# Two halves of an attention result leave apart and are added at the branch load; a one-column product moves from VectorE to GpSimd

## The chip, the cores and the metric

The kernel runs on one core of one Trainium2 chip. The metric is the device time of one execution, in microseconds. Of the kernel before, three runs gave 1775.21, 1780.83 and 1787.9 us; the median is 1780.83 us. One execution was profiled.

In the rows below PE is TensorE (matrix products), PEld its weight load, DVE is VectorE, ACT is ScalarE, POOL is GpSimd and SP is SyncE, whose queue issues nearly all transfers. L734 is line 734 of the kernel before.

## The reference, cut to what matters

One inference step of a one-layer encoder, for a prompt of 1024 tokens and a sample of 64 tokens: a norm and an input projection, stick-breaking attention beside a state-space branch, a gated merge of the two, an output projection, a gated feed-forward and an embedding stage. The change lies in the attention and where its result enters the merge:

```python
def _sb_block(qb, start, k, v, q_offset):
    z = jnp.einsum('bqhd,bkhd->bhqk', qb, k) * (SB_HEAD_DIM ** -0.5)
    ...
    visible = s_pos[None, :] < t_pos[:, None]
    log_keep = jnp.where(visible, jax.nn.log_sigmoid(-z), 0.0)
    after = lax.cumsum(log_keep, axis=3, reverse=True) - log_keep
    w = jnp.where(visible, jnp.exp(jax.nn.log_sigmoid(z) + after), 0.0)
    return jnp.einsum('bhqk,bkhd->bqhd', w, v)
...
merged = (jax.nn.sigmoid(g_attn) * (o_attn @ W['w_branch_attn'])
          + jax.nn.sigmoid(g_ssm) * (o_ssm @ W['w_branch_ssm']))
```

So a weight is sigmoid(z) times the product of sigmoid(-z) over all later visible keys. There are 8 heads of 64 columns each.

## The kernel before, in words

All matrix products are made in pieces: an operand is split into a high part (a ScalarE copy to a rounded type) and a low part (a VectorE subtraction), by `split` (L124 to L126) or `unit` (L102 to L115), and three products are added (`mm3_iter`, L137 to L139).

**Heads.** `head` walks the 1024 queries of one head in four groups `i2` of 256, each made of two tiles `i` of 128. The visible keys of groups 2 and 3 are taken in two parts, the later keys first. For each tile and part, `stick` lets ScalarE make p = sigmoid(-z) and w = sigmoid(z) from PSUM (L728, L729), VectorE scan p backwards into a running product (L730), and then w be multiplied by p shifted by one column (L732), on GpSimd for tile 0 and on VectorE for tile 1. The last column of a second part is multiplied by the carry, the running product of the part before it: a product of 128 partitions by one column, on VectorE (L734). The carry is a copy of column 0 of p (L737). `decode` does the same for the 64 sample tokens against 2048 cached keys, in five steps for each pair of heads, all of whose L732 are GpSimd's. In all there are 48 such one-column products: 32 of heads, 16 of `decode`.

The weights are then transposed by TensorE (L776) and split into wth and wtl (L780, L781). `weigh` (L806) multiplies them by values whose high and low parts lie side by side as 128 columns, so that a group's result `av` in PSUM has the high part's product in partitions 0 to 63 and the low part's in 64 to 127. ScalarE copies the upper half to `ot` (L719, from L792), VectorE adds it to the lower half into `o` (L793), and SP's queue writes `o` to the scratch `oad` of that pair of heads (L794). This happens 32 times. `av` has one PSUM bank, which `decode` uses too.

**Branch.** `branch` reads `oad` of one pair back (L918) into `braw`, a tile with one buffer, and splits it into `ba`. `early` does so for pairs 0 to 2 while the last heads run, each as one load of 1088 columns; `merge` does it for pair 3 in three chunks `CH` of 364, 362 and 362 columns, and then multiplies by the branch weights.

**Order.** A string, `ORDER`, written by a rule with fixed times, says in which order the heads, `decode` ("d"), the projections of the next pairs ("p"), the gate products that have no part in the attention ("g", `fill`) and `early` ("E") are put down. 48 further steps of gate products follow the last head. Matrix products of the fill may be held behind a given score product (`hold`). Within this, a planner that simulates the times of the engines (`schedule_with_timeline_sim=True`) fixes the order of the instructions on each engine; SP's queue, like each engine's, is worked off in that order.

Of the kernel before, what the change touches and what calls it, by code (L numbers as in the profile page):

```python
# [8 lines left out]
F32 = mybir.dt.float32  # L9
# [3 lines left out]
OP = mybir.AluOpType  # L13
# [4 lines left out]
SEQ = 1024  # L18
DEC = 64
TOK = SEQ + DEC  # L20
# [8 lines left out]
CH = ((0, 364), (364, 362), (726, 362))  # L29
# [39 lines left out]
class Net:  # L69
# [653 lines left out]
    def stick(self, P, z, n, carry, more, e):  # L723

        nc = self.nc
        w = P.tile([128, 512], F32, "w", "w")[:, :n]
        p = P.tile([128, 512], F32, "p", "p")[:, :n]
        nc.scalar.activation(p, z, AF.Sigmoid, scale=-1.0)  # L728
        nc.scalar.activation(w, z, AF.Sigmoid)  # L729
        nc.vector.tensor_tensor_scan(p[:, ::-1], p[:, ::-1], self.zero.to_broadcast([128, n]),  # L730
                                     1.0 if carry is None else carry, op0=OP.mult, op1=OP.add)
        (nc.gpsimd if e == 'g' else nc.vector).tensor_tensor(w[:, :n - 1], w[:, :n - 1], p[:, 1:], op=OP.mult)  # L732
        if carry is not None:
            nc.vector.tensor_tensor(w[:, n - 1:], w[:, n - 1:], carry, op=OP.mult)  # L734
        if more:
            carry = P.tile([128, 1], F32, "cy", "cy")
            nc.vector.tensor_copy(carry, p[:, 0:1])  # L737
        return w, carry

    def head(self, P, j, h, qs, ks, vs):  # L740

        nc = self.nc
        for i2 in range(4):
            nb = 2 * (i2 + 1)
            av = None
            parts = []
            carry = [None, None]
            m = (0, 0, 2, 4)[i2]
            for b0, b1 in ((m, nb), (0, m)) if m else ((0, nb),):
                ws = []  # L750
                for i in range(2):
                    qi = 2 * i2 + i
                    e1 = min(b1, qi + 1)
                    c0, n = b0 * 128, (e1 - b0) * 128
                    z = self.ps.tile([128, 512], F32, name="z", tag="z")[:, :n]
                    q = qs[:, qi * 128:(qi + 1) * 128]
                    last = b1 == nb
                    for r in range(2):
                        mile = nc.tensor.matmul(z, q, ks[:, r, c0:c0 + n], start=r == 0, stop=r == 1 and not last)
                    self.miles.append(mile)  # L760
                    if last:
                        nc.tensor.matmul(z[:, n - 128:], self.identb, self.neg, start=False, stop=True)
                    w, carry[i] = self.stick(P, z, n, carry[i], b0 > 0, EH[i])
                    ws.append(w)
                parts.append((b0, b1, ws))
            av = self.ps.tile([128, 512], F32, name="av", tag="av")[:, :256]
            done, late = 0, None
            for s0, s1, ws in parts:
                for b0 in range(s0, s1, 2):
                    ps = self.ps.tile([128, 512], F32, name="tr", tag="tr")  # L770
                    last = b0 + 2 == nb
                    for b in range(b0, b0 + 2):
                        for i, w in enumerate(ws):
                            if b <= 2 * i2 + i:
                                c = (b - b0) * 256 + i * 128
                                nc.tensor.transpose(ps[:, c:c + 128], w[:, (b - s0) * 128:(b - s0 + 1) * 128], self.ident)  # L776
                    wh = P.tile([128, 512], F32R, "wth", "wth")
                    wl = P.tile([128, 512], F32R, "wtl", "wtl")
                    for a, b in ((0, 256), (384, 512)) if last else ((0, 512),):
                        nc.scalar.activation(wh[:, a:b], ps[:, a:b], AF.Copy)  # L780
                        nc.vector.tensor_sub(wl[:, a:b], ps[:, a:b], wh[:, a:b])  # L781
                    todo = [late, (b0, last, wh, wl)]
                    if b0 + 2 < s1:
                        late = todo.pop()
                    else:
                        late = None
                    for x in todo:
                        if x:
                            done = self.weigh(av, vs, x, nb, done)
            ot = P.tile([64, 256], F32, "ot", "ot")  # L790
            o = P.tile([64, 256], F32, "o", "o")
            self.copy(EO, ot, av[64:128])  # L792
            nc.vector.tensor_add(o, av[:64], ot)  # L793
            nc.sync.dma_start(self.oad[j][h * 64:h * 64 + 64, i2 * 256:(i2 + 1) * 256], o)  # L794
            yield

    def weigh(self, av, vs, x, nb, done):
# [58 lines left out]
    def attention(self, P, PA, fill, early):  # L856

        self.oad = [self.dram.tile([128, TOK], F32, name=f"oad{j}") for j in range(4)]
        ops, self.miles = {}, []
        pa = PA.__enter__()  # L860
        for _ in self.project_pair(P, pa, 0, ops):
# [49 lines left out]
        yield from self.fm_iter(self.I["w_in"][0], n0, 8, evac, unit=unit)  # L911


    def branch(self, P, k, raw, chunks):

        b = P.pool.tile([128, 2, TOK], F32R, name=f"ba{k}")
        for c0, n in chunks:
            self.nc.sync.dma_start(raw[:, c0:c0 + n], self.oad[k][:, c0:c0 + n])  # L918
            self.split(b[:, 0, c0:c0 + n], b[:, 1, c0:c0 + n], raw[:, c0:c0 + n])
        return b  # L920

    def merge(self, P, B, raw):
        nc = self.nc

        def gates(m):
# [2 lines left out]
                nc.sync.dma_start(g[i], self.gd[8 * i + m])  # L928
            return g
        G = gates(0)  # L930
        B = B + [self.branch(P, 3, raw, CH)]
        for m in range(8):
            ga, gs = G
            if m < 7:
# [536 lines left out]
def body(tc, I, O, dbg=None, upto=99):  # L1471
    with ExitStack() as ctx:
# [58 lines left out]

        def early():

            p = pools(tc, "mrgA", dict(braw=1))
            mA.append(p)
            P = p.__enter__()
            for k in range(3):
                raw = P.tile([128, TOK], F32, "braw", "braw")
                Braw.append(N.branch(P, k, raw, ((0, TOK),)))

        PAA = pools(tc, "attA", dict(hl=2, qb0=1, qs0=2, raw=1, vs0=2, vn0=1, ob=2, kn0=1))
        with pools(tc, "att", dict(qs1=2, vs1=2, vn1=1, kn1=1, qb1=1, ks=3, w=6, p=3, cy=6, wth=2, wtl=2,
                                   ot=1, o=1, od=1, kr=1, vc=1, kk=1, wtd=1), "right") as P:
            N.ps.alias = {}
            N.attention(P, PAA, fill, early)
            with N.hold(1):
                fill(48)
# [7 lines left out]
        with pool("wout", "right") as PW:  # L1555
            N.HS = PW.tile([128, 8, 2 * DEC], F32R, name="HS")
            with pools(tc, "mrgB", dict(braw=1, ga=2, gs=2)) as P:
                raw = mA[0].tile([128, TOK], F32, "braw", "braw")
                N.merge(P, Braw, raw)
                U = N.mix_slabs(PW, 0, WO)  # L1560
            mA[0].__exit__(None, None, None)
            with pools(tc, "mix", dict(ss=4, xo=2, xn=2, xr=2, x0=1, x1=1, t1=1, t2=1)) as P:
                U += N.mix_slabs(P.pool, WO, 8)
                N.mix_out(P, U)
# [40 lines left out]
```

## Time and profile before

| | us |
|---|---|
| median of three runs | 1780.83 |
| the profiled execution's own time | 1778.77 |
| its span, first to last instruction | 1776.6 |
| attention, from the first score product to the last head's result | about 376 to 779 |
| product with the branch weights begins | 781 |

The profile has one row for each engine with its busy time, and views that cut the span into stages, list groups of instructions, list who waited for whom, and follow the chain of work that ended last. A busy TensorE is one that has a product under way; its granted clock stands beside it as a share of full speed. What a stage is worth is read from the stage, not from the mean of the span.

### The profile page before, as it was taken

The numbers are of one execution on the slowest core, as the hardware profiler recorded it, in microseconds if no ns is written. First come the engines' busy times: TensorE is split into PE (matmuls) and PEld (weight loads), VectorE is DVE, ScalarE is ACT, GpSimd is POOL, SyncE is SP. The second block draws the span as 40 slices with busy tenths as digits, with TensorE's granted clock in tenths as the row PEclk, the third lists the DMA queues.
The fourth block names the chain that finished last, engine by engine and source line by source line (L and its number), as shares of the span: only waits on it lengthen the run. The fifth ranks groups of instructions, "written<-read, shape, count | busy, mean of one in ns | idle before, by whom it ended". The sixth has DMA issues, their size and how long they took to land.

```text
span 1776.6 us, 24710 instructions
## 1 busy us (share of the span) xinstructions
PE 1692.9 (95%) x9092; PEld 1479.3 (83%) x9092; DVE 1039.0 (58%) x1581; ACT 733.5 (41%) x1357; POOL 515.3 (29%) x446
## 2 busy tenths in 40 slices
PE   8999897999999988899998999999999999999998
PEld 6999897988888877799786788888888887888886
DVE  6437735435776777767463655555655455445674
ACT  6431134124555555643343433343333344444542
POOL 2026100012322323224230444445444313001453
PEclk9999898999999999999999999999999999999999
DMA  8352534675343342147454444445444386655332
GB/s 283 95 147 64 120 89 149 216 213 137 88 101 101 83 118 83 60 143 239 143 172 148 132 149 133 160 132 187 151 149 139 125 288 215 197 189 166 107 113 89
DMA packets 220457, 258.23 MB, mean 145 GB/s; under 512 B 25888, under 2 KB 168336, under 8 KB 220320
## 3 DMA queue, kind: packets, MB, share of 16 engines
q1 hardware_dynamic: 219680, 255.20, 46.9%
q0 software_dynamic: 656, 1.44, 0.5%
q8 instruction: 72, 1.18, 0.3%
q14 instruction: 49, 0.40, 0.1%
HBM read 165.32 MB, written 76.51 MB: 136 GB/s over the span
## 4 chain that ended last, share of the span: by engine, by line
PE 73%; DVE 12%; DMA 7%; ACT 3%; issue 3%; SPq 1%; POOL 1%; DVEq 0%; POOLq 0%; ACTq 0%
PE pj L1200 13%; PE tr L1200 6%; PE pj L137 6%; PE pj L139 6%; PE pj L138 6%; PE z L1366 3%; DVE p L730 3%; PE z L1200 3%; PE pj L1366 3%; PE z L138 2%; PE z L139 2%; PE z L137 2%; PE tr L1366 2%; PE av L806 2%; PE tr L776 1%
## 5 line engine op out<-in xcount | busy, mean ns | idle before, releaser
L137 PE MATMUL pj<-H,wh 128*128 128x362 f32 (+3 forms) x648 | 217.7, 336 | 5.9 <-DVE ql L629 3.3
L139 PE MATMUL pj<-H,wl 128*128 128x362 f32 (+3 forms) x648 | 215.1, 333 | 0.6 <-DVE wl L115 0.6
L138 PE MATMUL pj<-H,wh 128*128 128x362 f32 (+3 forms) x648 | 214.6, 331 | 0.0
L126 DVE TENSOR_TENSOR wl<-raw,wh 128x1024 fp32r<-128x1024 f32 x96 | 132.3, 1380 | 120.0 <-ACT wh L125 118.7
L732 POOL TENSOR_TENSOR w<-w,p 128x383 f32<-128x383 f32 (+4 forms) x68 | 92.7, 1372 | 312.5 <-DVE w L734 185.2
L125 ACT ACTIVATE wh<-raw 128x1024 fp32r<-128x1024 f32 x96 | 101.4, 1059 | 122.8 <-PE z L1366 45.5
L137 PEld LDWEIGHTS pj<-H,wh 128*128 128x128 f32 x648 | 122.8, 190 | 7.6 <-DVE ql L629 3.7
L139 PEld LDWEIGHTS pj<-H,wl 128*128 128x128 f32 x648 | 122.5, 189 | 1.5 <-DVE wl L115 0.8
L138 PEld LDWEIGHTS pj<-H,wh 128*128 128x128 f32 x648 | 122.7, 189 | 0.9 <-issue 0.4
L1200 PE MATMUL pj<-H,s 128*128 128x512 f32 x480 | 118.2, 395 | 0.0
L148 POOL TENSOR_TENSOR rs<-rs,mhalf 128x1 f32<-128x1 f32 (+1 forms) x54 | 32.6, 605 | 278.0 <-DVE rs L147 277.9
L1200 PEld LDWEIGHTS pj<-H,s 128*128 128x128 f32 x480 | 89.9, 188 | 21.0 <-DVE c L1233 0.3
L125 ACT ACTIVATE s<-st 128x512 fp32r<-128x512 f32 x80 | 50.3, 629 | 123.6 <-PE pj L1200 112.2
L1134 POOL TENSOR_TENSOR st<-raw 128x512 f32<-128x512 f32 x40 | 60.7, 1518 | 133.8 <-DVE H L126 54.0
L126 DVE TENSOR_TENSOR s<-st,s 128x512 fp32r<-128x512 f32 x80 | 67.8, 849 | 39.4 <-ACT s L125 38.7
L119 ACT ACTIVATE wh<-raw 128x1024 fp32r<-128x1024 f32 (+1 forms) x52 | 46.8, 899 | 94.2 <-PE av L138 48.8
L780 ACT ACTIVATE wth<-tr 128x512 fp32r<-128x512 f32 (+2 forms) x112 | 50.2, 454 | 82.4 <-PE tr L776 41.9
L781 DVE TENSOR_TENSOR wtl<-tr,wth 128x512 fp32r<-128x512 f32 (+2 forms) x112 | 55.3, 496 | 49.3 <-ACT wth L780 48.9
L115 DVE TENSOR_TENSOR wl<-raw,wh 128x1024 fp32r<-128x1024 f32 (+1 forms) x50 | 51.1, 1021 | 55.0 <-ACT wh L119 54.9
L728 ACT ACTIVATE p<-z 128x512 f32<-128x512 f32 (+4 forms) x116 | 59.1, 510 | 42.6 <-PE z L830 16.7
L730 DVE TENSOR_TENSOR_SCAN p<-p,zero 128x384 f32<-128x384 f32 (+4 forms) x68 | 73.9, 1094 | 0.2
L1200 PE MATMUL pj<-H,wh 128*128 128x512 f32 x224 | 72.7, 401 | 0.6 <-ACT H L125 0.4
(553 smaller groups left out, 4630.2 us busy)
## 6 DMA issues: line engine op xcount, KB each, us to landing
sd<-c SPq DMA_DIRECT2D x77, 256.0 KB, 3.2
raw<-sd SPq DMA_DIRECT2D x77, 256.0 KB, 2.9
raw<-in_w_in_dram SPq DMA_DIRECT2D x32, 512.0 KB, 5.3
raw<-in_w_ffn_gate_dram SPq DMA_DIRECT2D x22, 512.0 KB, 3.6
raw<-in_w_ffn_up_dram SPq DMA_DIRECT2D x22, 512.0 KB, 5.1
wd<-in_w_ffn_down_dram SPq DMA_DIRECT2D x44, 256.0 KB, 3.3
td<-wd SPq DMA_DIRECT2D x22, 512.0 KB, 3.2
raw<-td SPq DMA_DIRECT2D x44, 256.0 KB, 3.0
```

Source lines behind the costliest of these rows:

```text
L125: self.nc.scalar.activation(wh, raw, AF.Copy)
L126: self.nc.vector.tensor_sub(wl, raw, wh)
L137: self.nc.tensor.matmul(out, wh, xh, start=i == 0, stop=False)
L138: self.nc.tensor.matmul(out, wh, xl, start=False, stop=False)
L139: self.nc.tensor.matmul(out, wl, xh, start=False, stop=i == n - 1)
L728: nc.scalar.activation(p, z, AF.Sigmoid, scale=-1.0)
L730: nc.vector.tensor_tensor_scan(p[:, ::-1], p[:, ::-1], self.zero.to_broadcast([128, n]), 1.0 if carry is None else carry, op0=OP.mult, op1 ...
L732: (nc.gpsimd if e == 'g' else nc.vector).tensor_tensor(w[:, :n - 1], w[:, :n - 1], p[:, 1:], op=OP.mult)
L781: nc.vector.tensor_sub(wl[:, a:b], ps[:, a:b], wh[:, a:b])
L1134: op(t, x, y)
L1200: self.nc.tensor.matmul(out, a[i][:, k], b[j][:, k], start=start and k == i == j == 0, stop=stop and k == 3 and i == 1, skip_group_check=n ...
L1366: nc.tensor.matmul(B[b + n], x[:, 0, c], y[:, 1], start=new and p == j == 0, stop=p == 10 and j == 2, skip_group_check=not new)
```

## The change

The result of a group leaves PSUM whole, by one ScalarE copy of 128 partitions, and its two halves go to two scratch tensors by two transfers; the VectorE addition in `head` is gone. `o` has two buffers, and `ot` is gone. `branch` loads both scratch tensors and adds them, in chunks of at most 512 columns; pairs 0 to 2 are loaded in two chunks instead of one. The second scratch has no sample columns. The tile `blow` that takes the second load has one buffer. Apart from this, the one-column product L734 is issued on GpSimd.

```diff
@@ stick
         if carry is not None:
-            nc.vector.tensor_tensor(w[:, n - 1:], w[:, n - 1:], carry, op=OP.mult)
+            nc.gpsimd.tensor_tensor(w[:, n - 1:], w[:, n - 1:], carry, op=OP.mult)
@@ head
-            ot = P.tile([64, 256], F32, "ot", "ot")
-            o = P.tile([64, 256], F32, "o", "o")
-            self.copy(EO, ot, av[64:128])
-            nc.vector.tensor_add(o, av[:64], ot)
-            nc.sync.dma_start(self.oad[j][h * 64:h * 64 + 64, i2 * 256:(i2 + 1) * 256], o)
+            o = P.tile([128, 256], F32, "o", "o")
+            self.copy(EO, o, av)
+            for i in range(2):
+                nc.sync.dma_start((self.oad, self.oal)[i][j][h * 64:h * 64 + 64, i2 * 256:(i2 + 1) * 256], o[i * 64:(i + 1) * 64])
@@ attention
+        self.oal = [self.dram.tile([128, SEQ], F32, name=f"oal{j}") for j in range(4)]
@@ branch
-    def branch(self, P, k, raw, chunks):
-
+    def branch(self, P, PB, k, chunks):
+
+        raw = PB.tile([128, TOK], F32, "braw", "braw")
         b = P.pool.tile([128, 2, TOK], F32R, name=f"ba{k}")
         for c0, n in chunks:
+            m = min(n, SEQ - c0)
             self.nc.sync.dma_start(raw[:, c0:c0 + n], self.oad[k][:, c0:c0 + n])
+            low = PB.tile([128, 512], F32, "blow", "blow")[:, :m]
+            self.nc.sync.dma_start(low, self.oal[k][:, c0:c0 + m])
+            self.nc.vector.tensor_add(raw[:, c0:c0 + m], raw[:, c0:c0 + m], low)
             self.split(b[:, 0, c0:c0 + n], b[:, 1, c0:c0 + n], raw[:, c0:c0 + n])
@@ early
-            p = pools(tc, "mrgA", dict(braw=1))
+            p = pools(tc, "mrgA", dict(braw=1, blow=1))
...
-                raw = P.tile([128, TOK], F32, "braw", "braw")
-                Braw.append(N.branch(P, k, raw, ((0, TOK),)))
+                Braw.append(N.branch(P, P, k, ((0, 512), (512, TOK - 512))))
@@ pools of the attention
-                                   ot=1, o=1, od=1, kr=1, vc=1, kk=1, wtd=1), "right") as P:
+                                   o=2, od=1, kr=1, vc=1, kk=1, wtd=1), "right") as P:
```

## Rows read from the trace of the kernel before

**Rows 1.** The page: busy time, share of the span and instructions of each engine.

```profile
PE 1692.9 (95%) x9092; PEld 1479.3 (83%) x9092; DVE 1039.0 (58%) x1581; ACT 733.5 (41%) x1357; POOL 515.3 (29%) x446
```

**Rows 2.** Stages: length, busy us of each engine, clock, DMA share, GB/s.

```profile
376.00:620.00 244.00, 231.36 (x1487) 212.78 (x1487) 164.01 (x296) 124.13 (x293) 70.42 (x66) 0.99 0.44 110
620.00:766.00 146.00, 126.57 (x778) 110.89 (x778) 114.21 (x202) 83.13 (x191) 42.76 (x37) 0.93 0.31 83
766.00:790.00 24.00, 24.00 (x157) 23.98 (x156) 10.54 (x19) 7.61 (x16) 2.63 (x3) 1.00 0.52 168
```

**Rows 3.** Chain of waits, 620 to 766 us: its shares by line.

```profile
by line: DVE p L730 27.6%; issue 8.1%; PE tr L776 7.1%; PE av L806 6.1%; DVE wtl L781 5.9%; DVE w L732 5.6%; PE z L830 4.4%; PE pj L137 4.2%; PE pj L138 3.8%; PE pj L139 3.7%; ACT wth L780 2.7%; ACT p L728 2.5%; DVE wl L115 2.4%; PE tr L824
```

**Rows 4.** Chain pieces of L793 by 40 us stretches, 376 to 776: start, us, what.

```profile
489.80 0.43 DVE o L793
...
755.19 0.06 DVE o L793
```

**Rows 5.** Groups by form, ScalarE, 376 to 782: copies of 256 columns from PSUM.

```profile
L780 ACT ACTIVATE wth<-tr 128x256 fp32r<-128x256 f32 x32 | 12.6, 394 | 14.4 <-PE tr L776 14.2
L719 ACT ACTIVATE ot<-av 64x256 f32<-64x256 f32 x32 | 12.2, 382 | 17.4 <-PE av L806 17.0
```

**Rows 6.** Groups by form, VectorE, 376 to 782: busy us, mean ns | idle before.

```profile
L732 DVE TENSOR_TENSOR w<-w,p 128x511 f32<-128x511 f32 x32 | 28.2, 881 | 1.5
L793 DVE TENSOR_TENSOR o<-av,ot 64x256 f32<-64x256 f32 x32 | 13.1, 408 | 7.3 <-ACT ot L719 7.2
L734 DVE TENSOR_TENSOR w<-w,cy 128x1 f32<-128x1 f32 x48 | 12.8, 267 | 0.0
```

**Rows 7.** Chain pieces of L734 by 40 us stretches, 376 to 776.

```profile
451.00 0.13 DVE w L734
...
735.47 0.90 DVE w L734
...
765.32 0.05 DVE w L734
```

**Rows 8.** Timeline, VectorE and GpSimd around 735 us.

```profile
734.21 1.27 DVE L730 TENSOR_TENSOR_SCAN p<-p,cy,zero 128x512 f32<-128x512 f32 x1
734.40 1.96 POOL L732 TENSOR_TENSOR w<-w,p 128x511 f32<-128x511 f32 x1 [3.43 <-ACT w L729]
735.40 0.97 DVE L734 TENSOR_TENSOR w<-w,cy 128x1 f32<-128x1 f32 x1
```

**Rows 9.** Groups by form, GpSimd, whole span: its shortest kinds of instruction.

```profile
L148 POOL TENSOR_TENSOR rs<-rs,mhalf 128x1 f32<-128x1 f32 x48 | 28.5, 594 | 243.7 <-DVE rs L147 243.6
L732 POOL TENSOR_TENSOR w<-w,p 128x63 f32<-128x63 f32 x4 | 1.2, 295 | 60.7 <-DVE p L730 60.7
L1594 POOL MEMSET const-float32-0.0<- 128x1 f32 x1 | 0.1, 99 | 0.2 <-issue 0.2
```

**Rows 10.** Line L732: who waited for it; us, times.

```profile
  ACT p L728: 13.7, 15
  PEld tr L776: 8.7, 5
```

**Rows 11.** Timeline, SP's queue: two loads of early branches, one of pair 3.

```profile
694.87 0.50 SPq L918 DMA_DIRECT2D braw<-oad  x1
...
707.32 0.34 SPq L918 DMA_DIRECT2D braw<-oad  x1
...
780.74 0.32 SPq L918 DMA_DIRECT2D braw<-oad  x1
```

**Rows 12.** Busy time in the stage 620 to 766: L734 alone, then L793 alone.

```profile
620.00:766.00 146.00, 5.80 (x22) 0.93 0.31 83
...
620.00:766.00 146.00, 5.32 (x13) 0.93 0.31 83
```

**Rows 13.** Groups by form, VectorE, 376 to 782: scans of 512 columns.

```profile
L730 DVE TENSOR_TENSOR_SCAN p<-p,cy,zero 128x512 f32<-128x512 f32 x32 | 43.1, 1350 | 24.5 <-ACT p L728 24.5
L730 DVE TENSOR_TENSOR_SCAN p<-p,zero 128x512 f32<-128x512 f32 x24 | 40.6, 1692 | 0.1
```

More of the change, by code (lines that the diff above doesn't have):

```diff
@@ L911, in columns, with merge @@
         yield from self.fm_iter(self.I["w_in"][0], n0, 8, evac, unit=unit)
-    def branch(self, P, k, raw, chunks):
+    def branch(self, P, PB, k, chunks):
+        raw = PB.tile([128, TOK], F32, "braw", "braw")
         b = P.pool.tile([128, 2, TOK], F32R, name=f"ba{k}")
         for c0, n in chunks:
+            m = min(n, SEQ - c0)
             self.nc.sync.dma_start(raw[:, c0:c0 + n], self.oad[k][:, c0:c0 + n])
+            low = PB.tile([128, 512], F32, "blow", "blow")[:, :m]
+            self.nc.sync.dma_start(low, self.oal[k][:, c0:c0 + m])
+            self.nc.vector.tensor_add(raw[:, c0:c0 + m], raw[:, c0:c0 + m], low)
             self.split(b[:, 0, c0:c0 + n], b[:, 1, c0:c0 + n], raw[:, c0:c0 + n])
         return b
-    def merge(self, P, B, raw):
+    def merge(self, P, B, PB):
         nc = self.nc
@@ L930, in merge @@
         G = gates(0)
-        B = B + [self.branch(P, 3, raw, CH)]
+        B = B + [self.branch(P, PB, 3, CH)]
         for m in range(8):
@@ L1557, in body @@
             with pools(tc, "mrgB", dict(braw=1, ga=2, gs=2)) as P:
-                raw = mA[0].tile([128, TOK], F32, "braw", "braw")
-                N.merge(P, Braw, raw)
+                N.merge(P, Braw, mA[0])
                 U = N.mix_slabs(PW, 0, WO)
```

## The prediction

> **What bounds the kernel now.** I read the page's busy times first, then the stages, then the chain of waits inside the stage that the change touches. The page says that TensorE is busy 95% of the span [rows 1], and the change takes no product away, so time can come only from TensorE's gaps or from its clock. The stages say where those are: from 376 to 620 us TensorE stands still for 244.0 - 231.4 = 12.6 us, from 620 to 766 us for 146.0 - 126.6 = 19.4 us at a granted clock of 0.93, and from 766 to 790 us not at all [rows 2]. VectorE is busy 114.2 of 146 us (78%) in the slow stretch, against 67% before it [rows 2]. The chain of waits agrees: there its largest entry is VectorE's scan with 27.6%, and the four VectorE entries among those shown make 27.6 + 5.9 + 5.6 + 2.4 = 41.5% [rows 3]. So work that VectorE loses or gains counts at about four tenths in the slow stretch and at little before it.
>
> **The sum, part by part.** It is made against the profiled execution, 1778.77 us (span 1776.6), which lies 2.1 below the median of the runs, 1780.83; I add 2.1 at the end.
>
> *The addition in the head goes.* It ran 32 times at 408 ns, 13.1 us of VectorE [rows 6]. What it gives back is what it holds of the chain: ten pieces between 376 and 776 us, which together are 3.3 us [rows 4]. Behind it stood the next use of the one bank of av. The rest ran beside other work, and that stays. Bounds: 0 (the next scan or split takes its place) and 13.1. I take -3.3, since the chain shows it directly.
>
> *The copy out of PSUM takes 128 partitions instead of 64.* A copy of the same 256 columns on 128 partitions took 394 ns, the one of 64 took 382 [rows 5]: 32 x 0.012 = 0.4 us of an engine with half its time free. Nothing. `o` is written one step earlier, and with two buffers the next copy waits for no transfer.
>
> *The one-column product leaves VectorE.* 48 x 267 ns = 12.8 us [rows 6]; on the chain it has 23 pieces, together 2.9 us [rows 7]. But 21 of them are short, and two long ones make 1.35 us of the 2.9. The one at 735.40 shows what a long one is: GpSimd's product began at 734.40 while VectorE's scan ran, took 1.96 us and ended at 736.36, and VectorE's one-column product, begun at 735.40, ended at 736.37 with it [rows 8]. It did no work for 0.97 us; it waited for GpSimd. The next product of two operands on VectorE would wait there instead. I therefore count only the short pieces, 2.9 - 1.35 = 1.55, rounded to -1.6; bounds 0 and -2.9.
>
> [...]
>
> *The one-column product arrives on GpSimd.* No row shows it. The nearest is the same kind of product on 63 columns, 295 ns; a fill of one column took 99 ns, and a power on one column 594 [rows 9]. I take 0.295, the same operation with the same kinds of operand, and keep 0.099 and 0.594: 48 x 0.295 = 14.2 us of GpSimd, which is busy 113 of 390 us in the attention [rows 2], so its time is free, its order is not. Queued behind it are GpSimd's wide products, and those are waited for by ScalarE 15 times (a buffer of p comes free) and by the transposes' weight loads six times with the five shown [rows 10]. Where the column stands ahead of the wide product in the queue and cannot be done while VectorE scans, the waiter loses 0.3. I take half of the 21: 21 x 0.5 x 0.295 = +3.1. Bounds: +1.0 (0.099 each) and +6.2 (0.594 each), each at half.
>
> *The addition arrives at the branch load.* Pairs 0 to 2 get two additions each, of 512 columns; the nearest VectorE row is 128x511 from SBUF, 881 ns [rows 6]: 6 x 0.88 = 5.3 us, and 0.5 for splits cut in two, an estimate. They fall between 695 and 745 us, in the slow stretch. At 41.5% of the chain [rows 3] that is 5.8 x 0.415 = +2.4; bounds 0 and +5.8.
>
> *The tail, pair 3.* Before, the last chunk was loaded at 780.74 [rows 11]. Now the last result leaves VectorE out, which gains 0.4, sends two stores instead of one and two loads instead of one, and adds 298 columns, some 0.5. That is about 1 us late in all. TensorE has products of the other pairs and other weight columns then, and stood still for none of 24 us [rows 2]. I put nothing; without that cover, +1.
>
> *SP's queue* gets 32 stores more, and eighteen loads (twelve early, six for pair 3) where there were six. They are hidden while nothing behind them is late; the case where it is stands below.
>
> Sum: 1778.8 - 3.3 - 1.6 + 3.1 + 2.4 = 1779.4; with the 2.1, **1781 us**: no change. VectorE is freed of 25.9 us and gets 7.2 back (three additions of pair 3 included, 1.4), but little of either lies on the path that sets the end.
>
> **The rivals.**
>
> *Freed VectorE time converts (faster).* For it: the slow stretch is VectorE's by the chain, and of the two removed steps 5.8 and 5.3 us lie in it [rows 12]. If all of that counts, less the 5.8 that come in, the gain there is 5.3; if half of the other 14.8 us counts before 620 us, 7.4 more. That is 12.7 us, 1768. Everything freed at once gives 25.9 - 7.2 = 18.7, 1762. Against it: before 620 us TensorE has only 12.6 us of gaps [rows 2], and the chain shows 6 us of the two steps, not 26.
>
> *GpSimd's column gets between the scans (slower).* Mechanism: the column waits for ScalarE's w and the old carry, both ready before the scan ends; put ahead of the wide product, it begins at the scan's end, the wide product follows, and VectorE's next scan waits for both, as VectorE's short product waited for GpSimd's at 735.40 [rows 8]. Place: between L730 and L730 of the same group. For it: a scan of 512 columns behind another scan, with GpSimd running, took 1.69 us on the mean, one of a second part 1.35 [rows 13]; GpSimd's product beside a scan took 1.96 [rows 8]. Price: 48 x 0.295 = 14.2, and 32 x (1.692 - 1.350) = 10.9, so 25.1 us of VectorE; at the chain's 41.5% it is 10.4 in place of the 3.1 above: 1780.9 - 4.9 + 2.4 + 10.4 = 1789. Paid in full, 1803. It decides where the planner puts the column ahead of the wide product in most groups. [...]
>
> *SP's queue stops behind `blow` (slower).* With one buffer, each second load waits until the addition of the chunk before is done, and the loads of cached keys and weights stand behind it. Before, one early load came 12.5 us after the other, since `braw` too has one buffer [rows 11]. Five such waits instead of two; if two key loads come 5 us late each and TensorE stops for them, +10, 1791. Against it: 86 us lie between the first early load and pair 3's last [rows 11], and the 20 decode steps of the 390 us come 20 us apart, so a key load has time.
>
> That the change doesn't do what it says, that is, that GpSimd's column delays VectorE as much as VectorE's own did, is inside the first case.
>
> **How the numbers follow.** No change 0.54, freed VectorE time 0.18, the column between the scans 0.16, SP's queue 0.12. The planner lays every engine's order out anew around the moved instructions; a few us either way from that are in each case. The three runs lie 0.7% apart, so about 1%, 18 us, is what can be told from no change. Below 1763 lies the end of the first rival and a lucky order, 0.11; above 1799 the full price of the second, an SP stall that goes on, and an unlucky order, 0.13; between, 0.76. The range 1766 to 1797 takes in the bounds of the sum (1780.9 - 13.1 - 2.9 + 1.0 = 1766, and 1780.9 + 6.2 + 5.8 + 1 = 1794), most of the first rival and the two slower ones at their usual price. The likeliest case alone is 1775 to 1787.
>
> **What would show it.** VectorE's busy time falls by some 19 us; L734 stands on GpSimd 48 times at about 0.3 us; the gaps of TensorE between 620 and 766 us stay near 19 us, and the scan stays at the head of the chain. The first rival: those gaps shrink to 10 or less. The second: scans of 512 columns of second parts lengthen from 1.35 toward 1.7. The third: SP's loads in early branches have long waits, and transposes of cached keys wait for a transfer. What would make the forecast wrong: a change of order that moves the fill's products out of the slow stretch, since then its gaps lie bare.

## The result, and the profile after

The changed kernel takes 1798.8 us, the median of four runs (1798.53 to 1799.56); the kernel before took 1781.14 beside it. The ratio is 1.009, its 95% interval 1.007 to 1.0111: slower by 0.9%, just inside the 1% that I called no change. The forecast of 1781 us was wrong, by 17.8 us, and the time lies 1.8 us above the range.

The page of the kernel after, busy time by engine, against [rows 1]:

```profile
PE 1703.7 (95%) x9092; PEld 1484.9 (83%) x9092; DVE 1036.4 (58%) x1513; ACT 732.1 (41%) x1360; POOL 539.4 (30%) x494
```

VectorE has 68 instructions fewer, and is busy 2.6 us less. I had forecast 19: what was taken from VectorE did not shorten its busy time by the sum of the durations, as the groups below show.

The stages of the kernel after (columns as in [rows 2]); the third runs to the first product with the branch weights, the fourth from there to the last:

```profile
376.00:620.00 244.00, 231.12 (x1469) 212.48 (x1468) 155.94 (x249) 120.74 (x288) 77.35 (x89) 0.98 0.48 117
620.00:766.00 146.00, 125.02 (x737) 108.06 (x736) 106.69 (x164) 78.89 (x182) 50.56 (x54) 0.92 0.38 102
766.00:792.70 26.70, 26.04 (x177) 24.94 (x176) 17.17 (x30) 13.26 (x31) 6.54 (x8) 1.00 0.21 63
792.70:847.50 54.80, 49.59 (x291) 47.80 (x290) 36.84 (x57) 17.96 (x38) 24.35 (x20) 1.00 0.69 221
```

TensorE stood still for 12.6 and 19.4 us in the first two stages before [rows 2]; now it stands still for 12.9 and 21.0. The new thing is in the last line: 5.2 us without a product, in a stage in which TensorE had never waited.

**A place, not a stage, is the better ruler.** Stages cut at fixed times hide a shift. The 32 results of the heads leave `av` in the same order in every kernel here, each by one ScalarE copy (L719), so I took the times of those copies as marks, numbered 0 to 31, and cut the trace at them. As the control I use not the profiled execution of the kernel before but that of a kernel with the same instructions in the same order on every engine, in which only the carry tile has one buffer more (experiment 1). It reached mark 0 at 411.0 us, the kernel before at 407.1, the kernel after at 410.5: the execution of before that was profiled was early by 4 us at the first head, for a reason outside the change, and so 3.4 us of the difference between the two profiles is no effect of it. From mark 3 on, before and control agree within 0.1 us from mark to mark.

Stretches of the control: marks 3 to 15, 15 to 16, 16 to 23, 23 to 31 (length, busy time of each engine, clock, DMA share, GB/s):

```profile
450.16:598.30 148.14, 142.66 (x932) 130.52 (x931) 109.26 (x197) 80.44 (x189) 47.17 (x45) 1.00 0.42 104
598.30:615.99 17.69, 14.98 (x104) 14.14 (x104) 14.10 (x22) 9.15 (x20) 5.01 (x4) 1.00 0.22 50
615.99:689.13 73.14, 63.15 (x394) 54.74 (x393) 53.46 (x102) 39.99 (x96) 22.60 (x22) 0.95 0.39 96
689.13:781.56 92.43, 82.99 (x514) 74.63 (x514) 70.60 (x118) 52.82 (x115) 23.04 (x17) 0.93 0.23 68
```

The same stretches of the kernel after:

```profile
449.71:599.19 149.48, 143.83 (x931) 131.08 (x931) 106.10 (x165) 80.38 (x190) 55.71 (x63) 1.00 0.44 108
599.19:618.27 19.08, 16.65 (x105) 15.79 (x105) 13.87 (x21) 9.15 (x20) 5.68 (x5) 0.91 0.22 49
618.27:691.47 73.20, 63.53 (x393) 54.93 (x392) 50.94 (x83) 39.69 (x96) 27.98 (x32) 0.95 0.42 102
691.47:790.08 98.61, 86.55 (x517) 76.87 (x517) 72.52 (x110) 52.76 (x118) 29.12 (x29) 0.91 0.30 90
```

The two spans lie 14.0 us apart (1797.1 and 1783.1), the medians 14.2 (1798.8 and 1784.6). By stretch: -0.5 to mark 3, +1.3, +1.4, +0.1, **+6.2** from mark 23 to 31, -0.3 from there to the first branch product, **+6.7** in the product stage, -0.9 behind it. Two places make 12.9 of the 14.0. In the product stage 5.2 of the 6.7 are gaps of TensorE; from mark 23 to 31 its gaps grow from 9.4 to 12.1 us, and the other 3.6 are longer busy time.

**Where the two steps went.** VectorE and GpSimd by form in the kernel after, 376 to 782 us, against [rows 6, 9, 13]; the third line has no counterpart shown there, it took 947 ns before:

```profile
L730 DVE TENSOR_TENSOR_SCAN p<-p,cy,zero 128x512 f32<-128x512 f32 x32 | 43.6, 1372 | 28.6 <-ACT p L728 28.6
L730 DVE TENSOR_TENSOR_SCAN p<-p,zero 128x512 f32<-128x512 f32 x24 | 34.1, 1423 | 0.1
L730 DVE TENSOR_TENSOR_SCAN p<-p,zero 128x384 f32<-128x384 f32 x24 | 32.9, 1370 | 0.0
...
L923 DVE TENSOR_TENSOR braw<-braw,blow 128x512 f32<-128x512 f32 x6 | 4.1, 682 | 5.4 <-DMA braw<-oad 4.9 <-DMA blow<-oal 0.5
...
L734 POOL TENSOR_TENSOR w<-w,cy 128x1 f32<-128x1 f32 x48 | 32.9, 686 | 174.0 <-ACT w L729 125.1 <-issue 48.6
```

One column costs GpSimd 686 ns, not 295. A timeline of the kernel after shows why, in one group of a head:

```profile
645.59 1.29 DVE L730 TENSOR_TENSOR_SCAN p<-p,cy,zero 128x512 f32<-128x512 f32 x1 [2.07 <-ACT p L728]
646.18 0.69 POOL L734 TENSOR_TENSOR w<-w,cy 128x1 f32<-128x1 f32 x1 [14.59 <-ACT w L729]
...
646.96 1.09 POOL L732 TENSOR_TENSOR w<-w,p 128x511 f32<-128x511 f32 x1
646.99 1.88 DVE L730 TENSOR_TENSOR_SCAN p<-p,zero 128x384 f32<-128x384 f32 x1
```

GpSimd's column begins at 646.18, while the scan runs, and ends at 646.87, with it (646.88). Of the 48, 22 end within 20 ns of the end of a scan, and 25 some 50 ns after the end of another VectorE operation on two tiles (L732 or L115); the one that met neither took 192 ns. So by estimate some 500 of the 686 ns are a wait for VectorE. The wide product follows at once and now lies beside the short scan, of 384 columns, which takes 1.88 us. So the pairing moved, as far as the means tell: the 384-column scan went from 947 to 1370 ns on the mean, and the first-part scan of 512 columns, which had GpSimd beside it before, from 1692 to 1423. What rival 2 described is there. What it costs, experiment 2 tells.

### The profile page after: what moved, and what is told of

Its sections match the earlier page's. It is cut to its first block, busy times and chain, and to the rows that moved or that the text cites. A ratio compares the mean times of both kernels' runs of the same rounds, so it can differ in the third digit from the quotient of the medians.

```text
span 1797.1 us, 24780 instructions
## 1 busy us (share of the span) xinstructions
PE 1703.7 (95%) x9092; PEld 1484.9 (83%) x9092; DVE 1036.4 (58%) x1513; ACT 732.1 (41%) x1360; POOL 539.4 (30%) x494
## 3 DMA queue, kind: packets, MB, share of 16 engines
q1 hardware_dynamic: 223968, 259.40, 47.9%
## 4 chain that ended last, share of the span: by engine, by line
PE 67%; DVE 15%; DMA 10%; issue 3%; ACT 2%; SPq 2%; POOL 1%; DVEq 0%; POOLq 0%; ACTq 0%
PE pj L1205 13%; PE tr L1205 6%; PE pj L137 5%; PE pj L139 5%; DVE p L730 5%; PE pj L138 5%; PE z L1371 3%; PE z L1205 3%; PE pj L1371 3%; PE tr L1371 2%; PE av L805 2%; PE z L137 2%; PE z L139 2%; PE z L138 2%; PE av L1371 1%
## 5 line engine op out<-in xcount | busy, mean ns | idle before, releaser
L732 POOL TENSOR_TENSOR w<-w,p 128x383 f32<-128x383 f32 (+4 forms) x68 | 82.9, 1223 | 129.9 <-DVE p L730 107.2
L734 POOL TENSOR_TENSOR w<-w,cy 128x1 f32<-128x1 f32 x48 | 32.9, 686 | 174.0 <-ACT w L729 125.1
L115 DVE TENSOR_TENSOR wl<-raw,wh 128x1024 fp32r<-128x1024 f32 (+1 forms) x50 | 51.3, 1027 | 57.8 <-ACT wh L119 57.7
L119 ACT ACTIVATE wh<-raw 128x1024 fp32r<-128x1024 f32 (+1 forms) x52 | 46.8, 899 | 92.3 <-PE av L138 46.3
L730 DVE TENSOR_TENSOR_SCAN p<-p,zero 128x384 f32<-128x384 f32 (+4 forms) x68 | 78.4, 1160 | 0.4 <-ACT p L728 0.2
```

## The experiments

A kernel's number behind the name is its ratio to the kernel before, timed on the same chip, with the 95% interval. All kernels are cut at the same marks (us, with the granted clock where it differs from 1.00; "product" is the stage from the first to the last product with the branch weights):

| kernel | 3 to 15 | 15 to 16 | 16 to 23 | 23 to 31 | product | span |
|---|---|---|---|---|---|---|
| before | 148.2 | 17.6 | 73.2 (.95) | 92.4 (.93) | 47.9 | 1776.6 |
| control (null_cy7) | 148.1 | 17.7 | 73.1 (.95) | 92.4 (.93) | 48.0 | 1783.1 |
| after | 149.5 | 19.1 (.91) | 73.2 (.95) | 98.6 (.91) | 54.7 | 1797.1 |
| halves_only | 148.8 | 17.4 | 72.7 (.95) | 98.4 (.91) | 54.5 | 1791.9 |
| column_only | 148.9 | 19.3 (.91) | 74.0 (.93) | 92.6 (.93) | 48.0 | 1783.9 |
| column_act | 148.1 | 19.1 (.91) | 74.2 (.93) | 91.9 (.94) | 47.9 | 1780.5 |
| halves_pair3 | 148.1 | 17.7 | 73.7 (.93) | 91.5 (.94) | 53.3 (.97) | 1785.1 |
| halves_pairs012 | 149.7 | 17.9 (.90) | 72.8 (.93) | 99.1 (.91) | 47.9 | 1790.0 |
| after_blow2 | 149.4 | 19.0 (.91) | 73.1 (.95) | 100.6 (.93) | 53.5 | 1798.1 |
| halves_whole | 148.8 | 17.4 | 72.6 (.95) | 96.1 (.95) | 55.6 (.97) | 1789.5 |
| halves_first | 148.9 | 18.9 (.91) | 74.7 (.91) | 98.2 (.91) | 47.9 | 1788.1 |
| early_split | 148.1 | 17.7 | 74.6 (.91) | 92.6 (.91) | 48.0 | 1779.9 |
| early_pool | 148.9 | 17.4 | 72.8 (.95) | 99.6 (.93) | 48.0 | 1785.1 |
| pair3_first_act | 148.1 | 19.1 (.91) | 73.9 (.93) | 91.1 (.94) | 48.0 | 1778.3 |

Each row is one execution. It lay within 1 us of its kernel's median, but for before (2.1 us below it), halves_pairs012 (4.3 us above it), halves_pair3 (3.3 below), halves_whole (4.3 below) and early_pool (2.8 below); there the stretches and the ratio need not add up.

**1. How much does no change move?** null_cy7: the kernel before, one buffer more for the carry.

```diff
-        ..., w=6, p=3, cy=6, ...
+        ..., w=6, p=3, cy=7, ...
```

> The kernel before with seven buffers instead of six for the carry, one column of four bytes. It changes no instruction and should change nothing: theories 1 and 2 expect 1778 to 1784. Theory 3 expects a new order and up to 6 us either way.

1.0006 (0.9991 to 1.0021): no difference. That allows it as the control.

**2. The two parts of the change by themselves.** halves_only is the kernel after with the column back on VectorE; column_only is the kernel before with the column on GpSimd; column_act is the kernel before with the column on ScalarE, which neither kernel does.

```diff
 halves_only (against after)
-            nc.gpsimd.tensor_tensor(w[:, n - 1:], w[:, n - 1:], carry, op=OP.mult)
+            nc.vector.tensor_tensor(w[:, n - 1:], w[:, n - 1:], carry, op=OP.mult)
 column_only (against before)
-            nc.vector.tensor_tensor(w[:, n - 1:], w[:, n - 1:], carry, op=OP.mult)
+            nc.gpsimd.tensor_tensor(w[:, n - 1:], w[:, n - 1:], carry, op=OP.mult)
 column_act (against before)
+            nc.scalar.activation(w[:, n - 1:], w[:, n - 1:], AF.Copy, scale=carry)
```

> The change with the one-column product put back on VectorE; the two halves, their stores, loads and additions stay. Theory 1 (the loss is the sum of three places: some 3 us from the column between the scans, some 6 us from the early branch loads between 700 and 760 us, some 7 us from pair 3's load and the product behind it): 1794 to 1797 us, 13 to 16 above before. Theory 2 (it is GpSimd's column alone): 1777 to 1783, as before. Theory 3 (it is the planner's new order, whatever was changed): no fixed sign, within 6 us of before.

> The kernel before with nothing changed but the one-column product, which GpSimd takes. Theory 1: 1782 to 1786 us, 1 to 5 above before, and no longer product stage than before's 48 us. Theory 2: 1795 to 1800. Theory 3: within 6 us of before, either sign. In each case the column takes about 0.7 us on GpSimd, most of it waiting for VectorE's scan.

> The kernel before with the one-column product on ScalarE (a copy scaled by the carry) instead of VectorE. [...] If the cost of moving the column is that it waits in another engine's order, it is as slow as with GpSimd, 1782 to 1786.

halves_only 1.0063 (1.0045 to 1.0082), column_only 1.0009 (0.9998 to 1.0021), column_act 0.9997 (0.9983 to 1.001). Most of the loss is the halves'. The column by groups, column_only first, column_act second:

```profile
L734 POOL TENSOR_TENSOR w<-w,cy 128x1 f32<-128x1 f32 x48 | 31.2, 650 | 169.6 <-ACT w L729 93.7 <-issue 75.5 <-PE z L759 0.2
```

```profile
L734 ACT ACTIVATE w<-w,cy 128x1 f32<-128x1 f32 x48 | 15.5, 324 | 0.7 <-DVE cy L737 0.6
```

On ScalarE it takes 324 ns, half as long, and waits for little but the carry; still nothing measurable comes back, nor is it slower: it takes 1782.8 us, where the kernel before took 1783.98 beside it. In the table column_only is longer than the control by 0.8 us from mark 3 to 15, at the same clock. The 1.6 us more from 15 to 16 come with a lower clock, 0.91 against 1.00, which column_act and halves_first share (last section). And VectorE, rid of 48 products that together lasted 12.8 us, is busy only 2.1 us less from mark 3 to 31 than in the control (column_only; 3.0 in column_act, where no column is GpSimd's): in the trace of the kernel before, ten of the 48, of 0.52 to 0.98 us each and 7.6 us together, end with an operation of GpSimd, as [rows 8] showed for one of them, and of the 5.3 us of the other 38, 4.5 lie under a neighbouring operation of VectorE.

**3. Which pairs' halves cost?** In halves_pair3 only pair 3 leaves as two halves, in halves_pairs012 only pairs 0 to 2; the others are added in `head` as before. The column is VectorE's in both. The tiles `ot` and `o` serve the halves in turn, as their two buffers.

```diff
+    def halves(self, j):
+        return j == 3          # halves_pairs012: j < 3
@@ head
+            if not self.halves(j):
+                ... (copy to ot, nc.vector.tensor_add(o, av[:64], ot), one store, as before)
@@ branch
-            low = PB.tile([128, 512], F32, "blow", "blow")[:, :m]
-            ...
+            if self.halves(k):
+                low = PB.tile([128, 512], F32, "blow", "blow")[:, :m]
+                ...
@@ early
+                Braw.append(N.branch(P, P, k, ((0, 512), (512, TOK - 512)) if N.halves(k) else ((0, TOK),)))
```

> The column stays on VectorE; only pair 3 leaves as two halves and is added at its load, pairs 0 to 2 keep the addition in the head and their one load each. Theory 1 now reads: of the halves' 11 us some 6 arise where the early branches load (700 to 760 us) and some 6.5 in the product with the branch weights. So here: the product stage takes 54 us instead of 47.5, heads 24 to 31 lose no more than 1 us against heads 0 to 23, and the time is 5 to 7 us above before. Rival (each store of a half, 64 more issues on SP, delays the heads themselves): a product of 47.5 us and no more than 3 us in all.

> The mirror: pairs 0 to 2 leave as halves and are added in the early branches, pair 3 keeps the addition in the head and three loads without one. Theory 1: the product stage is back at 47.5 us, heads 24 to 31 lose some 6 us against heads 0 to 23, time 4 to 7 us above before. Rival (the product is long because of what the early branches leave behind): product 54 us, 10 or more above.

halves_pair3 1.0035 (1.0023 to 1.0046), halves_pairs012 1.0022 (1.0008 to 1.0035). The table takes them apart: pair 3 makes the product stage longer by 5.3 us and no other stretch by more than 0.6; pairs 0 to 2 make the stretch from mark 23 to 31 longer by 6.7 (and the one from 3 to 15 by 1.6) and leave the product stage alone. So there are two losses at two places, and neither needs the other. By these two profiles they are of about the same size; by the ratios pair 3's is 6.2 us and that of pairs 0 to 2 is 3.9 (1.4 to 6.2). In halves_pair3 TensorE's gaps in the product stage are 2.9 us, and the rest comes at a granted clock of 0.97. The parts by themselves (0.35, 0.22 and 0.09%) make 0.66 of the 0.9%; by the intervals the rest is no firm remainder.

**4. Is it the one buffer of `blow`?** after_blow2 is the kernel after with two.

```diff
-            p = pools(tc, "mrgA", dict(braw=1, blow=1))
+            p = pools(tc, "mrgA", dict(braw=1, blow=2))
```

> The changed kernel with two buffers for the tile of the second load. If its single buffer is what costs (SP's queue stands until the addition before is done), 4 to 8 us come back: ratio 1.005 or less. If what costs is that ScalarE and VectorE, in their fixed order, wait for a load and for each other's part of every chunk, nothing or little comes back: ratio 1.007 to 1.010, and the product stays at 54 us.

1.01 (1.0072 to 1.0129), no better than the kernel after. From mark 23 to 31 it takes 100.6 us. Rival 3 is out.

**5. The product stage: one place in SP's queue.** In the kernel after, the loads of pair 3's last chunk (SP's queue, timeline):

```profile
792.43 0.33 SPq L920 DMA_DIRECT2D braw<-oad  x1
792.80 0.43 SPq L933 DMA_DIRECT2D ga<-gd  x1
793.33 0.38 SPq L933 DMA_DIRECT2D gs<-gd  x1
793.82 0.37 SPq L922 DMA_DIRECT2D blow<-oal  x1
```

The planner put two gate loads of 544 KB each between the high half and the low half. The low half, of 298 columns, has landed at 799.77, 5.95 us after its issue. Then, on VectorE, ScalarE and TensorE:

```profile
799.86 1.22 DVE L923 TENSOR_TENSOR braw<-braw,blow 128x298 f32<-128x298 f32 x1 [1.58 <-DMA blow<-oal]
801.11 0.51 ACT L125 ACTIVATE ba<-braw 128x362 fp32r<-128x362 f32 x1 [7.20 <-DVE braw L923]
...
806.24 0.43 PE L137 MATMUL z<-ba,wh 128*128 128x364 f32 x1 [1.22 <-ACT wh L119]
```

ScalarE works its queue off in order: it stands 7.20 us before the split of that chunk, and the splits of the next gate group's `H` and of the next branch weights (L119) stand behind it. TensorE then waits for a weight, not for the chunk. VectorE's queue stands behind the addition too. In the control the last load of pair 3 also goes out behind two gate loads; ScalarE waits at the same split for 3.43 us, and TensorE for nothing:

```profile
782.96 0.54 SPq L928 DMA_DIRECT2D ga<-gd  x1
783.59 0.40 SPq L928 DMA_DIRECT2D gs<-gd  x1
784.40 0.32 SPq L918 DMA_DIRECT2D braw<-oad  x1
...
789.29 0.51 ACT L125 ACTIVATE ba<-braw 128x362 fp32r<-128x362 f32 x1 [3.43 <-DMA braw<-oad]
```

Counted from the first product with the branch weights (784.69 in the control, 792.88 in the kernel after), this split begins after 4.6 us in the control and after 8.2 in the kernel after. halves_first changes one thing in the program: it is halves_only with `branch` of pair 3 put down ahead of the first gate loads.

```diff
@@ merge
-        G = gates(0)
         B = B + [self.branch(P, PB, 3, CH)]
+        G = gates(0)
```

> The halves with the column on VectorE; pair 3's loads are put down ahead of the first gate loads, so that on SP's queue the last chunk's second load stands right behind its first instead of behind two loads of 544 KB. If the product stage is 54 us instead of 48 because this load lands late and ScalarE waits in its order for the addition that needs it, with the weight splits behind it, the stage falls to 48 to 51 us and the ratio from 1.006 to 1.002 to 1.004. If it is the addition's own step on VectorE, or the larger number of loads, it stays at 54.

1.0034 (1.0019 to 1.0048), where halves_only had 1.0063. Its SP queue, and the split on ScalarE:

```profile
791.72 0.33 SPq L920 DMA_DIRECT2D braw<-oad  x1
792.40 0.33 SPq L922 DMA_DIRECT2D blow<-oal  x1
792.82 0.38 SPq L933 DMA_DIRECT2D ga<-gd  x1
...
795.66 0.51 ACT L125 ACTIVATE ba<-braw 128x362 fp32r<-128x362 f32 x1 [2.51 <-DVE braw L923]
```

The product stage is back at 47.9 us with TensorE busy through all of it:

```profile
792.00:839.90 47.90, 47.90 (x290) 47.90 (x289) 34.48 (x58) 17.31 (x39) 22.81 (x21) 1.00 0.78 257
```

The split now begins 3.5 us after the first branch product (792.12). The second load and the addition are still there, and the stores; putting pair 3's loads ahead of the gates gives back the 6.6 us of the stage. That is shown: the five kernels with pair 3 as halves behind the gates take 53.3 to 55.6 us here, all others 47.9 to 48.0, pair3_first_act (experiment 7) among them. The order alone is not the cause, for in the control it costs nothing. Order, second load and addition together make the split 3.6 us later than in the control, and that is more than the products at hand cover. How much of the lateness would have been harmless was not taken apart.

**6. The early branches.** What remains in halves_first is the other loss, from mark 23 to 31. Of it, most falls between marks 24 and 26; that stretch in the control and in the kernel after:

```profile
706.18:726.60 20.42, 20.21 (x130) 18.26 (x129) 16.89 (x31) 13.50 (x30) 5.36 (x4) 0.96 0.33 106
```

```profile
708.13:732.06 23.93, 20.93 (x130) 18.07 (x129) 17.83 (x32) 12.71 (x34) 6.19 (x7) 0.99 0.48 142
```

+3.5 us with the same 130 products at a clock that is no lower; TensorE's gaps grow from 0.2 to 3.0. From mark 26 to 28 another 2.5 come (22.9 to 25.4), at a clock of 0.77 against 0.85, with gaps of 4.6 against 4.3 us; whether that lower clock follows from the stops ahead of it is not shown. A timeline of the kernel after inside the first of the two:

```profile
711.70 0.60 ACT L728 ACTIVATE p<-z 128x512 f32<-128x512 f32 x1 [0.94 <-PE z L829]
713.61 0.69 DVE L923 TENSOR_TENSOR braw<-braw,blow 128x512 f32<-128x512 f32 x1 [3.66 <-DMA braw<-oad]
714.22 1.28 DVE L730 TENSOR_TENSOR_SCAN p<-p,cy,zero 128x512 f32<-128x512 f32 x1
...
719.50 0.68 DVE L923 TENSOR_TENSOR braw<-braw,blow 128x512 f32<-128x512 f32 x1
...
720.21 0.69 ACT L125 ACTIVATE ba<-braw 128x576 fp32r<-128x576 f32 x1 [2.29 <-DVE braw L923]
```

Two kinds of stop are to be seen. At 713.61 VectorE has stood 3.66 us for the load, with a scan of `decode` behind it whose p was ready at 712.30: it starts 1.9 us later. At 720.21 ScalarE has stood 2.29 us for an addition that came late in VectorE's queue. Before, the load went straight to ScalarE's split. Three variants ask which hop costs. halves_whole is halves_only with the early pairs loaded and added whole (one load, one addition of 1024 columns, one split); early_split is the kernel before with the early load and split cut into two chunks, with no second load and no addition; early_pool is halves_first with the early additions on GpSimd.

```diff
 halves_whole (against halves_only)
-            low = PB.tile([128, 512], F32, "blow", "blow")[:, :m]
+            low = PB.tile([128, SEQ], F32, "blow", "blow")[:, :m]
-                Braw.append(N.branch(P, P, k, ((0, 512), (512, TOK - 512))))
+                Braw.append(N.branch(P, P, k, ((0, TOK),)))
 early_split (against before)
-                Braw.append(N.branch(P, k, raw, ((0, TOK),)))
+                Braw.append(N.branch(P, k, raw, ((0, 512), (512, TOK - 512))))
 early_pool (against halves_first)
-            self.nc.vector.tensor_add(raw[:, c0:c0 + m], raw[:, c0:c0 + m], low)
+            (self.nc.gpsimd if k < 3 else self.nc.vector).tensor_add(raw[:, c0:c0 + m], raw[:, c0:c0 + m], low)
```

> Column on VectorE, halves for all pairs, but each early branch loads its two halves whole (1088 and 1024 columns) and adds and splits once: three chunks instead of six. Theory 1: of the 6 us between 700 and 760 some 2 to 4 come back, the product stays at 54 us, 7 to 10 above before. Rival (the additions' VectorE time itself, 4 us, is what costs there): nothing comes back, 11 above.

> The kernel before, but pairs 0 to 2 are loaded in two chunks of 512 and 576 columns, as after the change, without a second half and without an addition. If the early branches cost by the number of chunks that pass from load to ScalarE to VectorE, heads 24 to 31 lose some 3 us against heads 0 to 23 here. If it is the second load and the addition between load and split, they lose 1 us or less. The product stays at 48 us in both cases; ratio 1.000 to 1.002.

> Pair 3's loads first as in halves_first, and the additions of the early branches (pairs 0 to 2) on GpSimd instead of VectorE. If heads 24 to 31 lose some 6 us because VectorE, which has the scans, does 4 us of additions there and stands waiting for their loads, most of it comes back: heads 24 to 31 lose 2 us or less, ratio 1.000 to 1.002. If they lose it because ScalarE waits in its order for the addition, whichever engine makes it, they still lose 5 to 7 us, ratio 1.003 to 1.005. The product stays at 48 us.

halves_whole 1.0064 (1.0042 to 1.0086), early_split 1.001 (0.9996 to 1.0024), early_pool 1.0028 (1.0017 to 1.004). Cutting the load in two costs nothing by itself (92.6 us from mark 23 to 31). With the additions and half the hops the stretch is 3.7 us longer than the control's instead of 6.0; but TensorE's gaps in it are as long as in halves_only (11.7 and 11.9 us), the clock is higher (0.95 against 0.91), and by its time halves_whole is no faster. With the additions on GpSimd the stretch is 7.1 us longer, which is no help at all; but there the six take 9.7 us instead of 4.1, so this run does not part their work from their waits:

```profile
L923 POOL TENSOR_TENSOR braw<-braw,blow 128x512 f32<-128x512 f32 x6 | 9.7, 1617 | 20.1 <-DMA oal<-o 12.2 <-DMA braw<-oad 5.2 <-DMA blow<-oal 2.7
```

The waits for the branch between 700 and 790 us, ScalarE's and in the kernel after VectorE's too, in the control, in the kernel after and in early_pool (us in all, times, longest):

```profile
ACT ba L125 <- DMA braw<-oad: 4.9, 2, 3.4
```

```profile
ACT ba L125 <- DVE braw L923: 7.5, 5, 2.3
...
DVE braw L923 <- DMA braw<-oad: 4.9, 2, 3.7
DVE braw L923 <- DMA blow<-oal: 3.5, 2, 3.0
```

```profile
ACT ba L125 <- POOL braw L923: 10.0, 6, 3.8
```

What is shown is the place and the edit: the seven kernels that add the halves of pairs 0 to 2 at the load take 96.1 to 100.6 us from mark 23 to 31, the seven that do not take 91.1 to 92.6. The 4.1 us that the six additions last do not reach the 6.2, even if all of them lay on the path. What the waits point to, and no variant shows by itself, is that a step that waits for two transfers now stands between the load and the split, in queues that are worked off in order, and everything behind it waits as well, on two engines instead of one. How much of the 6 us belongs to the additions' work, to VectorE's stop, to ScalarE's and to the second load stays open.

**7. What the experiments point to.** pair3_first_act leaves only pair 3 as halves, with its loads ahead of the gates, and puts the column on ScalarE (the rest of `halves` as in halves_pair3).

```diff
+    def halves(self, j):
+        return j == 3
-            nc.gpsimd.tensor_tensor(w[:, n - 1:], w[:, n - 1:], carry, op=OP.mult)
+            nc.scalar.activation(w[:, n - 1:], w[:, n - 1:], AF.Copy, scale=carry)
@@ merge
-        G = gates(0)
         B = B + [self.branch(P, PB, 3, CH)]
+        G = gates(0)
```

> What the runs so far leave over as harmless, put together: only pair 3 leaves as halves, its loads stand ahead of the gate loads, and the one-column product is ScalarE's. Heads 24 to 31 should lose nothing, the product should take 48 us, and the time should be that of before, 0.998 to 1.001: VectorE is freed of some 13 us, of which nothing but 0 to 3 us lies on the path.

0.9984 (0.9971 to 0.9997), 1780.58 us against 1783.61: about 3 us faster than the kernel before, just outside the noise, and, by the two ratios, about 1% faster than the kernel after. Where they arise is not shown: from mark 3 to the end of the product stage its profile takes 382.7 us, the control's 382.6. From mark 23 to 31 it takes 91.1 us where the control takes 92.4, as halves_pair3 took 91.5. But column_act, without any halves, takes 91.9 at the same clock of 0.94, so at most 0.4 to 0.8 us of this can be the last pair's addition, and single profiles do not show so little.

## Why the prediction was wrong, point by point

**The tail, pair 3: the step that failed.** I put nothing, "without that cover, +1". The stage became 6.7 us longer, and two terms were wrong. The lateness, "about 1 us in all", was 3.6 to 3.7: counted from the last group's store, the last load goes out 1.35 us later than in the control (793.82 - 790.49 against 784.40 - 782.42), takes 1.1 longer to land (5.95 against 4.9), and the addition and its hand-over put in 1.3. I priced the loads as if each went out when it was wanted, and never asked which transfers the planner could put between the two halves. And the cover was not free of the delay: I did not ask who stands behind the split on ScalarE, and it is the weights for the very products that I named as cover.

**The additions at the early loads: mis-sized.** I took +2.4, with 5.8 as the bound. The duration, 0.88 us each, was if anything high (682 ns). The stretch lost 6.2, more than the bound. The share of the chain, 41.5%, was the wrong multiplier: it priced the addition as work alone, though it waits, for two transfers, at the head of VectorE's queue, and ScalarE then waits for it. That is the question "what is queued behind the waiting instruction", which I answered for GpSimd's column and not for this one. That these waits make the difference is argued from the trace, not shown (experiment 6).

**The addition gone from `head`: -3.3, and it did not come.** With halves_only the three stretches before the early branches, marks 3 to 23, take 238.9 us against 239.0 in the control. The ten chain pieces of L793 [rows 4] were real, but the lower bound, 0, was the value; probably another wait ends at the same time where they vanish, which no run shows.

**The column off VectorE and onto GpSimd: -1.6 + 3.1.** The sum, +1.5, was near what column_only measured, +0.09% or 1.6 us (-0.02 to 0.21%), but that is luck: both are within the noise, and the parts were wrong. column_act, which frees VectorE as well, gave 0.03% and not 1.6 us, again within the noise. GpSimd's column lasted 686 ns and not 295, above the upper bound of 594, because it waits for VectorE. I had read in [rows 8] that VectorE's column waited for GpSimd's product; I could have asked there whether GpSimd's column would wait for VectorE's scan. The column's and the scan's ends at 646.87 and 646.88 show that it did in that group. That the next product on VectorE would wait for GpSimd in the column's place, for which I left the two long pieces (1.35 us) out of the -1.6, was my estimate from [rows 8]; no run shows it.

**The rivals.** Freed VectorE time does not convert: TensorE's gaps before 620 and from 620 to 766 us did not shrink. GpSimd's column does get between the scans, nearly as rival 2 says, though in other scans than its sign named: those of second parts stayed at 1372 ns, and the 384-column ones grew. But it costs some 1.6 us (at most 0.21%, 3.7 us) and not 10: by the means, a scan that is lengthened at one place is shortened at another. SP's queue had a part in the product stage, though not by the one buffer of rival 3: a second load that goes out late, with an addition behind it, was enough.

**The signs.** The scan is at the head of the chain from 620 to 766 us, as said (27.6% before [rows 3]):

```profile
by line: DVE p L730 31.4%; issue 9.4%; PE av L805 8.0%; PE tr L776 7.1%; DVE w L732 5.4%; PE z L829 5.0%; DVE wtl L781 4.6%; ACT p L728 2.5%; DVE braw L923 2.3%; DMA braw<-oad 2.3%; PE pj L137 2.2%; DVE wl L115 2.2%; DMA blow<-oal 1.8%; PE 
```

The new entries, L923 and its two loads, have 6.4% together: 9 us of a stretch of 146, where the sum had 2.4. Two signs failed: VectorE's busy time fell by 2.6 us and not by 19, and the column takes 686 ns and not 300.

## What to carry to other kernels

When a sum is moved from the producer to the load, price the load's queue and not the addition alone: ask what the scheduler can put between the two transfers, and what stands behind the step that now waits for both, on each engine that is worked off in order. Put small loads that a product needs ahead of large ones that can wait; here one line's place was worth 6.6 us of a stage. Gate loads ahead of this load had cost nothing before the change, so ask anew when a step is added behind it. And compare places in the program with a control that has the same instructions: 4 us of the difference between two single profiles lay ahead of the change.

## What the runs showed of the hardware

Between marks 15 and 16 some kernels take 17.4 to 17.7 us at the full clock, and others 18.9 to 19.3 (halves_pairs012: 17.9) at 0.90 or 0.91. halves_only and halves_first have the same order of products on TensorE up to the product stage; after the same gap, in which TensorE is busy for 0.23 of 2 us, one goes on at the full clock and the other at half of it. From the start of that gap, in pieces of 2 us, halves_only:

```profile
604.27:606.27 2.00, 0.23 (x3) 0.00 (x0) 2.00 (x4) 1.53 (x4) 0.34 (x2) 1.00 0.37 101
606.27:608.27 2.00, 1.52 (x12) 1.55 (x13) 1.96 (x5) 0.60 (x1) 0.78 (x1) 1.00 0.10 30
```

and halves_first:

```profile
603.59:605.59 2.00, 0.23 (x3) 0.00 (x0) 2.00 (x4) 1.52 (x4) 0.34 (x2) 1.00 0.39 113
605.59:607.59 2.00, 1.49 (x10) 1.52 (x11) 1.96 (x5) 0.59 (x1) 0.81 (x1) 0.85 0.06 18
607.59:609.59 2.00, 2.00 (x8) 2.00 (x8) 2.00 (x5) 0.28 (x2) 0.00 (x0) 0.50 0.00 0
```

From mark 15 to 16 halves_first takes 18.93 us and halves_only 17.35. Why the clock falls behind the gap in the one and not in the other, no run shows. Seven of the fourteen profiles have the fall, among them all five with the column off VectorE and two of the nine with it on VectorE. Whether moving the column makes the fall likelier was not tried.
